# Shorter candidate lists and bf16 steps in the expert routing, forty instead of thirty-two slots taken beside the dense products, one pool to each weight and row buffer

## The chip, the cores and the metric

The kernel runs on one core of one Trainium2 chip. The metric is device time in microseconds (us) of one execution: 1737.02 us, the median of three runs (1736.02 to 1741.25). Smaller is better.

## The reference, cut to what matters

The program is three transformer layers over 256 tokens of width 1024. The change lies wholly in the last sublayer, a product-key expert layer, and in the two pool lines that all layers use:

```python
def peer_ffn(h, w_q, sub_keys, u, v):          # 256 tokens, 8 heads, 128 keys per half, 16384 experts
    q = (hf @ w_q).reshape(n, PEER_HEADS, 2, PEER_HALF)
    sc = jnp.einsum('nhcd,hckd->nhck', q, sub_keys)
    s_top, i_top = lax.top_k(sc, PEER_TOPK)                                   # 16 of 128, per half
    cand_s = s_top[:, :, 0, :, None] + s_top[:, :, 1, None, :]                # 16 x 16 pair sums
    cand_i = i_top[:, :, 0, :, None] * PEER_N_KEYS + i_top[:, :, 1, None, :]
    best_s, pos = lax.top_k(cand_s.reshape(n, PEER_HEADS, 256), PEER_TOPK)    # the 16 best pairs
    best_i = jnp.take_along_axis(cand_i.reshape(n, PEER_HEADS, 256), pos, axis=-1)
    g = jax.nn.softmax(best_s, axis=-1)
    # 128 slots (8 heads x 16) per token; for each token and slot e:
    a = gelu(h . u[e]) * g ;  out = sum over slots of a * v[e]
```

## The kernel before, in words

Everything up to the expert layer is a chain of matrix products whose weights stream from HBM in blocks of 128 x 1024 fp32 (512 KB). `fetch` starts the load of a block into a "raw" buffer from SyncE's queue; `split` makes a rounded copy `whi` on ScalarE (L444) and the rest `wlo` on VectorE (L445, or L293 where VectorE's order is kept); `mm3` (L383 to L385) multiplies both. The raw and `whi`/`wlo` buffers come from two pools that `weight_pools` opens, one with three raw buffers and one with three pairs at the time of the expert layer.

The expert layer (`peer_stage`) has two stages.

**The dense stage.** `nblocks` runs 128 blocks "u" on TensorE: the products of all tokens with all 16384 rows of the table u, laid into a 128 KB per partition `grid` (ScalarE, L1528). After each block `tick` advances two generators by one step each. `paced` advances `routes`: for each of 8 heads `routing` finds the 16 best of 128 for both halves (MAX8, FIND_INDEX8, MATCH_REPLACE8), forms 256 pair sums, takes the 16 best pairs, and turns their positions into key indices by an equality compare, a multiply and a reduce over 1024 elements each (two token halves x 16 picks x 2 halves x 16 candidates); after the eighth head `gates` follows. `two_heads` takes slots 0 to 31 (heads 0 and 1) of the first 128 tokens out of turn: for each slot GpSimd gathers 128 rows of u by index (`row_load`, L1548, one indirect DMA of 512 KB), VectorE forms the dot product, and later the row of v is gathered and added into `peerq`. Row n is due at block 13 + 1.5 n, so 64 rows are spread over blocks 13 to 109. Their buffers are seven quarter rows of the grid that no product has reached yet; four of them are given up at block 96. On VectorE all of this stands in program order (`_InOrder`, L293) with the splits.

**The row stage.** `expert_sums` closes the weight pools and opens its own in their place: six row buffers `vrow` in one pool, then `oj`, `junk` and small tiles. What is left are the v rows of all slots but those 32: 128 loads "o" in groups of four (step n = 0 to 31; each row there is for one slot of 64 tokens twice), 64 loads "u" of token half 1 and 32 of half 0. In step n, `second` builds one-hot columns (L1702 on TensorE, L1704 on VectorE), `weights` picks the dot products out of the grid (L1716 on TensorE, L1722 on VectorE) and applies the gelu, `add` sums four rows on TensorE (L1740); from n = 16 on four "u" units follow, three as a multiply-add on VectorE (L1762), the fourth as a diagonal product on TensorE (ScalarE L1757 makes the diagonal, TensorE L1759). After step 30 `turn(0)` (L1750) makes the weights of half 0, and the last 32 units run, 22 on VectorE and 10 on TensorE. `close` normalizes and writes one token half. Loads are issued by GpSimd in one fixed order, as soon as one of 12 row buffers (two in `xres`, six `vrow`, four in the tiles `xh` and `xl`) is free; eight more come out of the grid after every eighth step.

Of the kernel before, what the change touches and what calls it, by code (L numbers as in the profile page):

```python
# [212 lines left out]

_CONST = [("ident", 128), ("ones", 128), ("iota", 128)]
_CONST2 = [("ones64", 128), ("perm1", 128), ("perm2", 128), ("tri", 128), ("wmask", 256), ("gla", 7 * 128)]


def _constants():
    i = np.arange(128)
    c = {}  # L220
    c["ident"] = np.eye(128)
    c["ones"] = np.ones((128, 128))
    c["iota"] = np.tile(i[None, :], (128, 1))
    c["ones64"] = (i[:, None] // 64 == i[None, :] // 64) * 1.0
# [24 lines left out]
    b = np.concatenate([c[n] for n, _ in _CONST2], axis=1).astype(np.float32)  # L249
    return np.ascontiguousarray(a), np.ascontiguousarray(b)  # L250
# [45 lines left out]
class _Kernel:  # L296
# [355 lines left out]
    def run(self):  # L652
# [16 lines left out]
        nc.vector.memset(self.eps, EPS)  # L669
        self.ident, self.ones, self.iota = c1[:, 0:128], c1[:, 128:256], c1[:, 256:384]  # L670

# [784 lines left out]
    def peer_stage(self):  # L1456
        nc, tc = self.nc, self.tc
        with ExitStack() as s:
# [65 lines left out]
            self.dve = _InOrder(tc, nc.vector)  # L1524
            self.start(self.paced(routes(), 0.68))
            self.start(self.two_heads(p1, base, own, htok, rcol, tok, q, xd))
# [7 lines left out]

    def paced(self, gen, rate):

        n = t = 0
        while True:
            t += 1
            while n < max(min(t, 10), t * rate):  # L1540
                if next(gen, self) is self:
                    return
                n += 1
            yield

    def row_load(self, out, table, idx):

        self.nc.gpsimd.indirect_dma_start(out, None, self.A[table], bass.IndirectOffsetOnAxis(ap=idx, axis=0))  # L1548

    def two_heads(self, p1, base, own, htok, rcol, tok, q, xd):  # L1550


        v = self.dve
        idx = p1.tile([128, 32], U32, name="idx0")
        gate = p1.tile([128, 32], F32, name="gate0")
        a = p1.tile([128, 32], F32, name="act0")
        sm = p1.tile([128, 2], F32, name="gsum0")
        acc = q[:, 0:4].rearrange("p k t -> p (k t)")
# [3 lines left out]
        loaded = ready = 0  # L1562
        first, pace = 13, 1.5

# [3 lines left out]
        def load():  # L1568
            nonlocal loaded
            while loaded < 64:  # L1570
                if loaded < 32 and ready <= loaded // 16:
                    return
                end = first + 1 + pace * loaded
# [4 lines left out]
                n = loaded % 32  # L1578
                self.row_load(at[loaded][1], "pu" if loaded < 32 else "pv", idx[:, n : n + 1])
                loaded += 1  # L1580
# [18 lines left out]

        for n in range(64):  # L1600
            while True:
                prepare()
                if self.scored >= 4 and not begun:
                    begun = True
                    self.nc.gpsimd.dma_start(acc, xd[:, 0:D])
                if block() >= first + pace * n and (ready > n // 16 if n < 32 else self.scored >= 4):
                    break
# [4 lines left out]
            assert block() < end, (n, block(), end)  # L1612
            if n < 32:
                v.scalar_tensor_tensor(row, row, 1.0, htok, op0=OP.mult, op1=OP.mult, accum_out=a[:, n : n + 1])
            else:
                v.scalar_tensor_tensor(acc, row, a[:, n - 32 : n - 31], acc, op0=OP.mult, op1=OP.add)
            if used:
                free.append(used)
            used = end, row
            if n == 31:  # L1620
                v.tensor_scalar(a, a, rcol[:, 0:1], None, op0=OP.mult)
# [4 lines left out]
    def expert_sums(self, s, grid, own, slot, idxp, idxt, jrow, sums, xd):  # L1626
# [144 lines left out]
        for n in range(32):  # L1771
# [11 lines left out]
            if n >= 16:  # L1783
                for k in range(4 * (n - 16), 4 * (n - 16) + 4):
                    unit(1, k, k % 4 == 3)
                    load()
        for k in range(32, 64):
            unit(0, k, k % 3 == 1)
            load()
            if k == 40:  # L1790
                self.close(1, sums, acc[0], free.pop(0))
# [33 lines left out]
    def routing(self, p2, h, q, tok, left):  # L1825

        nc = self.nc
        v = self.dve
# [15 lines left out]
        it = p2.tile([128, 2, 2, 16], U32, tag="rit", bufs=1, name=self.name("rit"))  # L1844
        itf = p2.tile([128, 2, 2, 16], F32, tag="ritf", bufs=1, name=self.name("ritf"))
        for c, tt in pairs:
# [38 lines left out]
        pf = p2.tile([128, 2, 16, 2], F32, tag="pf", bufs=1, name=self.name("pf"))  # L1885
        v.tensor_single_scalar(pij[:, :, :, 0], pos, 4, op=OP.logical_shift_right)
        v.tensor_single_scalar(pij[:, :, :, 1], pos, 15, op=OP.bitwise_and)
        v.tensor_copy(pf, pij)
        yield

        eq = self.x[:, 0:4].rearrange("p n t -> p (n t)")
        v.tensor_tensor(eq.rearrange("p (m b) -> p m b", b=16),
                        pf.rearrange("p t k c -> p (t k c)").unsqueeze(2).broadcast_to([128, 64, 16]),
                        self.iota[:, 0:16].unsqueeze(1).broadcast_to([128, 64, 16]), op=OP.is_equal)
# [81 lines left out]
```

## Time and profile before

| | |
|---|---|
| median of three runs | 1737.02 us |
| profiled execution: its own time / its span | 1743.55 / 1741.8 us |
| dense stage of the expert layer | about 985 to 1358 us of the span |
| row stage | 1358 to 1742 us |
| TensorE busy in the dense / the row stage to 1689 us | 99% / 63% |
| DMA share in the same two | 0.73 / 0.93 |

The profile is that of one execution, which took 6.5 us more than the median. Times in rows are us from the span's start, durations of one instruction ns or us as the row says. Two instructions in a row on VectorE overlap by some 0.08 us, so durations added up come out a few per cent above the time they take. "Remote" and "issue" name idle time of an engine for which the profile shows no releaser.

### The profile page before, as it was taken

What the parts mean: (1) busy time and instruction counts of PE and PEld (TensorE: products, weight loads), DVE (VectorE), ACT (ScalarE), POOL (GpSimd) and SP (SyncE); (2) the same over time, 40 slices, a digit from 0 to 9 for tenths busy, and PEclk for the clock granted to TensorE, in tenths of its full rate; (3) what the DMA queues carried; (4) which work ended last, traced back from release to release, by engine and by line L of the source; (5) the groups of instructions that cost most, each with busy time, mean ns of one, the idle gap of its engine ahead of it and who ended that gap; (6) DMA issues with size and microseconds to landing.
All of it is one profiled execution on the core that took longest, in us unless ns stands there. A gap on an engine that the chain in (4) does not pass through costs nothing.

```text
span 1741.8 us, 31524 instructions
## 1 busy us (share of the span) xinstructions
PE 1568.8 (90%) x12094; PEld 1423.6 (82%) x12094; DVE 1354.2 (78%) x2929; ACT 846.7 (49%) x1522; POOL 340.4 (20%) x313
## 2 busy tenths in 40 slices
PE   6999999999999999999999999999999756674656
PEld 6999999988999999898998999999999534342322
DVE  7859888897788888888776789999994546664657
ACT  7546555755665558348756555555556100000002
POOL 0000000000000000000000043344220466676670
PEclk9999999999999999999999999999999979776868
DMA  6446555424465554443554688877865699998991
GB/s 233 136 146 197 187 185 182 161 96 158 141 199 184 187 188 160 137 145 100 179 180 151 240 329 297 308 252 250 278 232 204 236 348 326 342 356 336 352 377 32
DMA packets 108711, 380.07 MB, mean 218 GB/s; under 512 B 12288, under 2 KB 16896, under 8 KB 108432
## 3 DMA queue, kind: packets, MB, share of 16 engines
q1 hardware_dynamic: 64640, 223.20, 38.6%
q0 software_dynamic: 41760, 152.06, 23.7%
q10 hardware_dynamic: 2160, 2.79, 0.5%
q8 instruction: 95, 1.56, 0.4%
q14 instruction: 56, 0.46, 0.1%
HBM read 375.91 MB, written 2.10 MB: 217 GB/s over the span
## 4 chain that ended last, share of the span: by engine, by line
PE 77%; DVE 11%; issue 5%; another core or an unknown queue 4%; ACT 2%; DMA 1%; DVEq 0%; ACTq 0%
PE mm L383 17%; PE mm L385 17%; PE mm L384 17%; PE acc L384 4%; PE acc L383 4%; PE acc L385 4%; PE mm L1716 3%; DVE junk L1722 3%; DVE peerq L1762 2%; PE acc L1740 2%; PE acc L1759 1%; DVE oj L1704 1%; DVE wlo L293 1%; PE acc L611 1%
## 5 line engine op out<-in xcount | busy, mean ns | idle before, releaser
L383 PE MATMUL mm<-xh,whi 128*128 128x256 f32 x2536 | 724.1, 286 | 5.6 <-DVE z L882 2.7
L385 PE MATMUL mm<-xh,wlo 128*128 128x256 f32 x2536 | 716.8, 283 | 2.2 <-DVE wlo L293 2.1
L384 PE MATMUL mm<-xl,whi 128*128 128x256 f32 x2536 | 717.1, 283 | 0.2 <-DVE xl L492 0.2
L444 ACT CAST whi<-raw 128x1024 fp32r<-128x1024 f32 x366 | 383.1, 1050 | 393.8 <-PE mm L384 197.5
L383 PEld LDWEIGHTS mm<-xh,whi 128*128 128x128 f32 x2536 | 483.2, 191 | 12.7 <-DVE z L882 3.1
L385 PEld LDWEIGHTS mm<-xh,wlo 128*128 128x128 f32 x2536 | 483.6, 191 | 4.3 <-DVE wlo L293 2.9
L384 PEld LDWEIGHTS mm<-xl,whi 128*128 128x128 f32 x2536 | 484.1, 191 | 1.7 <-DVE xl L492 0.6
L445 DVE TENSOR_TENSOR wlo<-raw,whi 128x1024 fp32r<-128x1024 f32 x291 | 354.8, 1223 | 98.0 <-ACT whi L444 95.7
L1716 PE MATMUL mm<-grid,oj 128*128 128x128 f32 x512 | 85.6, 326 | 97.9 <-issue 43.2
L1548 POOL DMA_INDIRECT grid<-in_pu,idx x32 | 50.4, 1574 | 603.5 <-DMA keys<-in_keys 537.6
L1716 PEld LDWEIGHTS mm<-grid,oj 128*128 128x128 f32 x512 | 75.9, 231 | 106.4 <-issue 67.2
L374 ACT ACTIVATE a<-a 128x8 f32<-128x8 f32 x32 | 6.7, 210 | 257.6 <-DVE a L1724 120.3
L1722 DVE SCALAR_TENSOR_TENSOR junk<-c1t,slotT,mm 128x128 f32<-128x128 f32 x256 | 88.7, 346 | 49.7 <-remote 21.1
L293 DVE TENSOR_TENSOR wlo<-raw,whi 128x1024 fp32r<-128x1024 f32 x75 | 91.2, 1222 | 23.7 <-ACT whi L444 23.6
L384 PE MATMUL acc<-fl,whi 128*128 128x256 f32 x352 | 98.9, 281 | 0.1
L385 PE MATMUL acc<-fh,wlo 128*128 128x256 f32 x352 | 98.5, 280 | 0.0
L383 PE MATMUL acc<-fh,whi 128*128 128x256 f32 x352 | 97.7, 279 | 0.0
L1704 DVE TENSOR_SCALAR oj<-mm,cols 128x512 f32<-128x512 f32 x64 | 45.8, 747 | 61.3 <-remote 33.2
L444 ACT CAST whi<-grid 128x1024 fp32r<-128x1024 f32 x51 | 53.8, 1054 | 63.1 <-PE mm L384 51.6
L1528 ACT COPY grid<-mm 128x256 f32<-128x256 f32 x128 | 80.5, 629 | 5.9 <-PE mm L385 5.9
L1548 POOL DMA_INDIRECT grid<-in_pv,idx x32 | 63.0, 1968 | 99.6 <-DVE peerq L293 79.1
L1548 POOL DMA_INDIRECT vrow<-in_pv,idxp x60 | 60.1, 1001 | 68.6 <-PE mm L385 37.4
(415 smaller groups left out, 2748.2 us busy)
## 6 DMA issues: line engine op xcount, KB each, us to landing
raw<-in_wts SPq DMA_DIRECT2D x366, 512.0 KB
grid<-in_wts SPq DMA_DIRECT2D x51, 512.0 KB
mem<-in_mem SPq DMA_DIRECT2D x8, 128.0 KB
xspill<-grid ACTq DMA_DIRECT2D x1, 1024.0 KB
peerq<-xspill POOLq DMA_DIRECT2D x2, 512.0 KB
out<-grid SPq DMA_DIRECT2D x4, 256.0 KB
vrow<-in_pv,idxp POOLq DMA_INDIRECT x60
grid<-in_pv,idxt POOLq DMA_INDIRECT x60
```

What stands on the lines that cost most here:

```text
L293: return lambda *a, **kw: self.tc.keep_in_program_order(f(*a, **kw))
L383: mm(ps, lhsT=wh, rhs=xh, start=first, stop=False, skip_group_check=True)
L384: mm(ps, lhsT=wh, rhs=xl, start=False, stop=False, skip_group_check=True)
L385: mm(ps, lhsT=wl, rhs=xh, start=False, stop=last, skip_group_check=True)
L444: self.nc.scalar.copy(hi, x)
L445: self.dve.tensor_tensor(lo, x, hi, op=OP.subtract)
L1528: lambda i, ps: nc.scalar.copy(grid[:, :, :, :, i // 16, i % 16], ps.rearrange("p (t c r) -> p t c r", t=2, c=8)))
L1548: self.nc.gpsimd.indirect_dma_start(out, None, self.A[table], bass.IndirectOffsetOnAxis(ap=idx, axis=0))
L1704: v.tensor_scalar(oj[:, h], ps, ip, None, op0=OP.is_equal)
L1716: keep(nc.tensor.matmul(ps[:, c].rearrange("p (q i) -> p q i", q=8), lhsT=oj[:, h, c], rhs=grid[:, tt, 2 * c + h, r], start=True, stop=True))
L1722: v.scalar_tensor_tensor(junk, self.iota, slot[:, 0, t : t + 1], bank[h][:, c], op0=OP.is_equal, op1=OP.mult, accum_out=a[:, h, c : c + 1])
L1740: keep(nc.tensor.matmul(acc[n // 16][hf][32 * c : 32 * c + 32], lhsT=strips[n % 3][:, c, 31 - r : 63 - r], rhs=rows[c][:, hf * 512 : hf * ...
```

## The change

Four things change. (1) `routing` forms only the pair sums that can be among the best 16: all 16 partners for the first 4, the first 4 for the other 12, so 112 instead of 256, and the searches read 112. Positions become indices by sums of index steps: `dif` holds the differences of successive indices in bf16, the compare is "position at or past the start of candidate b" against a new constant `cuts` (fp32 in, bf16 out), the multiply and the reduce read bf16. Two conversions leave VectorE, and three stand on ScalarE instead. (2) `two_heads` takes 40 slots in place of 32, 80 rows, one every 1.4 blocks to block 35 and one every 1.08 after that; `paced` gives the routing 0.76 of a step per block, then 0.5, and 1.25 from block 104. The row stage loses 8 units of half 0. Two small tiles move into a constant. (3) Each weight buffer and each `vrow` gets a pool of its own; the `vrow` pools are opened last, so that they lie on the three pairs, and are used in the order in which those come free. (4) Row loads keep their program order on GpSimd.

```diff
     def weight_pools(self, stack, raw_bufs, hl_bufs, side="left"):
-        raw = stack.enter_context(self.tc.tile_pool(name=self.name("wraw"), bufs=raw_bufs, side=side))
-        hl = stack.enter_context(self.tc.tile_pool(name=self.name("whl"), bufs=hl_bufs, side=side))
-        self.wraw = self.wraw + [raw] * raw_bufs
-        self.whl = self.whl + [hl] * hl_bufs
+        for pools, n, name in ((self.wraw, raw_bufs, "wraw"), (self.whl, hl_bufs, "whl")):
+            pools += [stack.enter_context(self.tc.tile_pool(name=self.name(name), bufs=1, side=side)) for _ in range(n)]
...
-            while n < max(min(t, 10), t * rate):
+            while n < max(min(t, 10), min(10 + 0.76 * (t - 10), 29 + 0.5 * (t - 35)), 63.5 + 1.25 * (t - 104)):
...
-        self.nc.gpsimd.indirect_dma_start(out, None, self.A[table], bass.IndirectOffsetOnAxis(ap=idx, axis=0))
+        self.tc.keep_in_program_order(self.nc.gpsimd.indirect_dma_start(
+            out, None, self.A[table], bass.IndirectOffsetOnAxis(ap=idx, axis=0)))
...
-        first, pace = 13, 1.5
+        def when(n):
+            return 13 + 1.4 * n if n < 16 else 35.4 + 1.08 * (n - 16)
...
-        for n in range(64):
+        for n in range(80):
...
-        free = xrows + [pv.tile([128, D], F32, name=f"vrow{i}") for i in range(6)]
+        pw.tile([128, 40], F32, name="pad")
+        vrows = [s.enter_context(tc.tile_pool(name=f"pv{i}", bufs=1, side="right")).tile(
+            [128, D], F32, name=f"vrow{i}") for i in range(6)]
+        free = xrows + [vrows[2 * ((self.wi + j) % 3) + i] for j in range(3) for i in range(2)]
...
-        units = {1: [(1, k) for k in range(64)], 0: [(0, k) for k in range(32, 64)]}
+        units = {1: [(1, k) for k in range(64)], 0: [(0, k) for k in range(40, 64)]}
...
-        for k in range(32, 64):
-            unit(0, k, k % 3 == 1)
+        for k in range(40, 64):
+            unit(0, k, k % 3 == 2)
...
+        dif = p2.tile([128, 2, 2, 16], BF16, tag="rdif", bufs=1, name=self.name("rdif"))
...
-        for tt in range(2):
-            v.tensor_tensor(cand[:, tt].rearrange("p (a b) -> p a b", a=16),
-                            st[:, tt, 0].unsqueeze(2).broadcast_to([128, 16, 16]),
-                            st[:, tt, 1].unsqueeze(1).broadcast_to([128, 16, 16]), op=OP.add)
+        for a0, a1, b1, p0, p1 in ((0, 4, 16, 0, 64), (4, 16, 4, 64, 112)):
+            shape = [128, 2, a1 - a0, b1]
+            v.tensor_tensor(cand[:, :, p0:p1].rearrange("p t (a b) -> p t a b", b=b1),
+                            st[:, :, 0, a0:a1].unsqueeze(3).broadcast_to(shape),
+                            st[:, :, 1, 0:b1].unsqueeze(2).broadcast_to(shape), op=OP.add)
+        cand = cand[:, :, 0:112]
...
-        v.tensor_copy(itf, it)
+        nc.scalar.copy(itf[:, :, :, 1:17], it)
...
+        v.tensor_tensor(dif, itf[:, :, :, 1:17], itf[:, :, :, 0:16], op=OP.subtract)
...
-        v.tensor_copy(pf, pij)
+        nc.scalar.copy(pf[:, :, :, 0], pos)
+        nc.scalar.copy(pf[:, :, :, 1:3], pij)
...
+        v.scalar_tensor_tensor(pf[:, :, :, 2], pf[:, :, :, 0], 64.0, pf[:, :, :, 2], op0=OP.is_ge, op1=OP.mult)
+        v.tensor_tensor(pf[:, :, :, 1], pf[:, :, :, 1], pf[:, :, :, 2], op=OP.subtract)
+        eq = self.x[:, 0:2].rearrange("p n t -> p (n t)").bitcast(BF16)
...
-        v.tensor_tensor(e4, e4, itf.rearrange("p t c b -> p t (c b)").unsqueeze(2).broadcast_to([128, 2, 16, 32]),
+        v.tensor_tensor(e4, e4, dif.rearrange("p t c b -> p t (c b)").unsqueeze(2).broadcast_to([128, 2, 16, 32]),
```

GpSimd's instructions where the dense stage ends, before (`xres`, `vrow` and `grid` are places of row buffers; the buffers `vrow` 16946 to 16951 are the six of the one pool, 16952 and 16953 lie in `xh` and `xl`):

```order
L1765 DMA peerq<-xspill 128x1024
L1548 DMA grid<-in_pv,idx_12255 128x1024 x6
L1548 DMA xres<-in_pv,idxp 128x1024 x2
L1548 DMA vrow_16953<-in_pv,idxp 128x1024
L1647 MEMSET strip_16938 128x252
L1647 MEMSET strip_16939 128x252
L1647 MEMSET strip_16940 128x252
L1548 DMA vrow_16946<-in_pv,idxp 128x1024
```

The same place now (17027 to 17047 are the six `vrow` buffers, a pool each):

```order
L1549 DMA grid<-in_pv,idx_12289 128x1024 x40
L1774 DMA peerq<-xspill 128x1024
L1549 DMA xres<-in_pv,idxp 128x1024 x2
L1652 MEMSET strip_17015 128x252
L1652 MEMSET strip_17016 128x252
L1652 MEMSET strip_17017 128x252
L1549 DMA vrow_17027<-in_pv,idxp 128x1024
```

A row of the twelfth buffer no longer stands ahead of the first `vrow` loads, and the 40 loads of v rows of the dense stage stand in one piece.

VectorE's last units before the second `close`, before:

```order
L1751 SCALAR_TENSOR_TENSOR wsmall<-mm_18960,cols,wsmall 128x64
L1762 SCALAR_TENSOR_TENSOR peerq<-grid,wsmall,peerq 128x1024 x3
L1762 SCALAR_TENSOR_TENSOR peerq<-xres,wsmall,peerq 128x1024
L1802 TENSOR_TENSOR peerq<-peerq,acc_17071 128x512
...
L1762 SCALAR_TENSOR_TENSOR peerq<-grid,wsmall,peerq 128x1024 x14
```

The same now:

```order
L1760 SCALAR_TENSOR_TENSOR wsmall<-mm_19048,cols,wsmall 128x64
L1771 SCALAR_TENSOR_TENSOR peerq<-grid,wsmall,peerq 128x1024 x3
L1771 SCALAR_TENSOR_TENSOR peerq<-xres,wsmall,peerq 128x1024
L1811 TENSOR_TENSOR peerq<-peerq,acc_17167 128x512
...
L1771 SCALAR_TENSOR_TENSOR peerq<-grid,wsmall,peerq 128x1024 x8
```

From the weights of half 0 on, 25 multiply-adds stood on VectorE, and 19 stand there now; six of them are gone from the last run.

## Rows read from the trace of the kernel before

**Rows 1.** Busy time by stretch (length, then busy us and instructions of each engine, then TensorE's granted clock, DMA share and GB/s): the dense stage, 24 us early in it, its blocks 35 to 104, and two parts of the row stage.

```profile
985.00:1358.00 373.00, 370.89 (x3093) 368.30 (x3091) 330.19 (x705) 210.76 (x296) 117.25 (x68) 1.00 0.73 258
1020.00:1044.00 24.00, 24.00 (x202) 24.00 (x202) 22.49 (x62) 12.89 (x17) 9.93 (x7) 1.00 1.03 409
1090.00:1289.00 199.00, 198.12 (x1652) 196.25 (x1651) 195.73 (x416) 110.89 (x148) 77.06 (x44) 1.00 0.78 271
1358.00:1505.00 147.00, 94.76 (x736) 57.42 (x734) 85.71 (x371) 12.41 (x58) 88.97 (x96) 0.86 0.90 326
1505.00:1689.00 184.00, 113.20 (x609) 61.50 (x609) 109.69 (x322) 14.98 (x56) 126.94 (x126) 0.75 0.95 352
```

**Rows 2.** TensorE's waits in the dense stage (us in total, times, longest).

```profile
PE mm L385 <- DVE wlo L293: 2.1, 4, 1.2
```

**Rows 3.** Two splits on VectorE late in the dense stage, where nothing else stands on it (start, us).

```profile
1341.97 1.23 DVE L293 TENSOR_TENSOR wlo<-raw,whi 128x1024 fp32r<-128x1024 f32 x1 [1.66 <-ACT whi L444]
1344.85 1.23 DVE L293 TENSOR_TENSOR wlo<-raw,whi 128x1024 fp32r<-128x1024 f32 x1 [1.65 <-ACT whi L444]
```

**Rows 4.** VectorE's groups in the dense stage by form (count, busy us, mean ns, idle before). FIND_INDEX8, MAX8 and MATCH_REPLACE8 search; 128x256 are the pair sums.

```profile
L293 DVE TENSOR_TENSOR wlo<-raw,whi 128x1024 fp32r<-128x1024 f32 x75 | 91.2, 1222 | 23.7 <-ACT whi L444 23.6
L293 DVE TENSOR_TENSOR wlo<-grid,whi 128x1024 fp32r<-128x1024 f32 x51 | 62.1, 1224 | 5.3 <-ACT whi L444 5.1 <-issue 0.2
L293 DVE SCALAR_TENSOR_TENSOR peerq<-grid,act,peerq 128x1024 f32<-128x1024 f32 x32 | 41.0, 1280 | 0.0
L293 DVE SCALAR_TENSOR_TENSOR grid<-grid 128x1024 f32<-128x1024 f32 x32 | 39.0, 1219 | 0.1
L293 DVE FIND_INDEX8 rit<-rst,xres 128x8 uint32<-128x128 f32 x64 | 17.5, 294 | 0.0
L293 DVE MAX8 rst<-xres 128x8 f32<-128x128 f32 x64 | 14.3, 287 | 5.0 <-ACT xres L1842 5.0
L293 DVE FIND_INDEX8 pos<-xres 128x8 uint32<-128x256 f32 x32 | 13.1, 424 | 0.0
L293 DVE MAX8 xres<-xres 128x8 f32<-128x256 f32 x32 | 12.0, 418 | 0.0
L293 DVE TENSOR_TENSOR xres<-xres,ritf 128x1024 f32<-128x1024 f32 x8 | 9.8, 1220 | 0.0
L293 DVE TENSOR_TENSOR xres<-pf,c1t 128x1024 f32<-128x1024 f32 x8 | 9.8, 1219 | 0.0
L293 DVE TENSOR_REDUCE xres<-xres 128x64 f32<-128x1024 f32 x8 | 9.7, 1216 | 0.0
L293 DVE MATCH_REPLACE8 xres<-rst,xres 128x128 f32<-128x128 f32 x32 | 8.7, 282 | 0.0
L293 DVE MATCH_REPLACE8 xres<-xres 128x256 f32<-128x256 f32 x16 | 6.5, 414 | 0.0
L293 DVE TENSOR_TENSOR xres<-rst 128x256 f32<-128x256 f32 x16 | 6.1, 431 | 0.0
L293 DVE TENSOR_TENSOR xres<-xres,gmx 128x128 f32<-128x128 f32 x2 | 0.6, 292 | 0.1
```

**Rows 5.** GpSimd's row loads around the end of the dense stage, in order of time.

```profile
1317.95 1.27 POOL L1548 DMA_INDIRECT xres<-in_pv,idxp  x1 [26.04 <-PE mm L385]
...
1358.41 0.99 POOL L1548 DMA_INDIRECT vrow<-in_pv,idxp  x1 [37.38 <-PE mm L385]
...
1370.34 0.94 POOL L1548 DMA_INDIRECT vrow<-in_pv,idxp  x1 [0.30 <-issue]
```

**Rows 6.** VectorE at the second step of the row stage, in order of time.

```profile
1366.88 0.17 DVE L1724 TENSOR_TENSOR a<-a,rs 128x8 f32<-128x8 f32 x1
1371.08 0.35 DVE L1722 SCALAR_TENSOR_TENSOR junk<-c1t,slotT,mm 128x128 f32<-128x128 f32 x1 [4.03 <-remote]
```

**Rows 7.** TensorE at the same place: the picks of step 1 and the first sum of rows.

```profile
1364.72 2.05 PE L1716 MATMUL mm<-grid,oj 128*128 128x128 f32 x16 [0.27 <-DVE junk L1722]
1372.11 1.07 PE L1740 MATMUL acc<-xres,strip 128*32 128x512 f32 x2 [5.34 <-issue]
```

**Rows 8.** The largest unexplained waits of the row stage (us in total, times, longest).

```profile
PE mm L1716 <- issue: 43.2, 9, 15.2
...
DVE oj L1704 <- remote: 33.2, 6, 15.9
```

**Rows 9.** VectorE at the end, in order of time: the weights of half 0, the last run of units, the second close.

```profile
1688.83 0.28 DVE L1750 TENSOR_SCALAR wsmall<-mm,cols 128x64 f32<-128x64 f32 x1 [7.64 <-PE acc L1740]
...
1697.47 0.69 DVE L1802 TENSOR_TENSOR peerq<-peerq,acc 128x512 f32<-128x512 f32 x1 [3.01 <-PE acc L1759]
...
1711.35 18.46 DVE L1762 SCALAR_TENSOR_TENSOR peerq<-grid,wsmall,peerq 128x1024 f32<-128x1024 f32 x14
1729.91 1.29 DVE L1802 TENSOR_TENSOR peerq<-peerq,acc 128x512 f32<-128x512 f32 x2
```

**Rows 10.** TensorE at the end: the last two diagonal products.

```profile
1722.81 1.98 PE L1759 MATMUL acc<-grid,wsmall 128*128 128x512 f32 x4 [0.55 <-ACT wsmall L1757]
1725.35 1.98 PE L1759 MATMUL acc<-grid,wsmall 128*128 128x512 f32 x4 [0.55 <-ACT wsmall L1757]
```

**Rows 11.** GpSimd at the end: the first and the last of the final 32 row loads.

```profile
1650.21 0.94 POOL L1548 DMA_INDIRECT xres<-in_pv,idxt  x1 [0.30 <-issue]
...
1694.38 0.94 POOL L1548 DMA_INDIRECT grid<-in_pv,idxt  x1 [0.31 <-issue]
```

More of the change, by code (lines that the diff above doesn't have):

```diff
@@ L210, in _pack_small @@
     return np.ascontiguousarray(np.concatenate([parts[k].astype(np.float32) for k, _ in _SMALL], axis=1))
-_CONST = [("ident", 128), ("ones", 128), ("iota", 128)]
+_CONST = [("ident", 128), ("ones", 128), ("iota", 128), ("cuts", 32)]
 _CONST2 = [("ones64", 128), ("perm1", 128), ("perm2", 128), ("tri", 128), ("wmask", 256), ("gla", 7 * 128)]
@@ L223, in _constants @@
     c["iota"] = np.tile(i[None, :], (128, 1))
+    k = np.arange(16)
+    c["cuts"] = np.tile(np.concatenate([np.where(k < 4, 16 * k, 48 + 4 * k), k])[None, :], (128, 1))
     c["ones64"] = (i[:, None] // 64 == i[None, :] // 64) * 1.0
@@ L669, in run @@
         nc.vector.memset(self.eps, EPS)
-        self.ident, self.ones, self.iota = c1[:, 0:128], c1[:, 128:256], c1[:, 256:384]
+        self.ident, self.ones, self.iota, self.cuts = (c1[:, a:b] for a, b in ((0, 128), (128, 256), (256, 384), (384, 416)))
         with ExitStack() as s1:
@@ L1524, in peer_stage @@
             self.dve = _InOrder(tc, nc.vector)
-            self.start(self.paced(routes(), 0.68))
+            self.start(self.paced(routes()))
             self.start(self.two_heads(p1, base, own, htok, rcol, tok, q, xd))
@@ L1533, in peer_stage, with paced @@
             self.expert_sums(s, grid, own, slot, idxp, idxt, jrow, q.rearrange("p (t k) n -> p t (k n)", t=2), xd)
-    def paced(self, gen, rate):
+    def paced(self, gen):
         n = t = 0
@@ L1546, in row_load @@
     def row_load(self, out, table, idx):
-        self.nc.gpsimd.indirect_dma_start(out, None, self.A[table], bass.IndirectOffsetOnAxis(ap=idx, axis=0))
+        self.tc.keep_in_program_order(self.nc.gpsimd.indirect_dma_start(
+            out, None, self.A[table], bass.IndirectOffsetOnAxis(ap=idx, axis=0)))
     def two_heads(self, p1, base, own, htok, rcol, tok, q, xd):
         v = self.dve
[L1554 to L1557, printed above, removed]
+        idx = p1.tile([128, 48], U32, name="idx0")
+        gate, a, sm = self.ones[:, 0:48], self.ones[:, 48:96], self.ones[:, 96:99]
         acc = q[:, 0:4].rearrange("p k t -> p (k t)")
@@ L1569, in load @@
             nonlocal loaded
-            while loaded < 64:
-                if loaded < 32 and ready <= loaded // 16:
+            while loaded < 80:
+                if loaded < 40 and ready <= loaded // 16:
                     return
-                end = first + 1 + pace * loaded
+                end = when(loaded) + 1
                 k = next((k for k, (b, _) in enumerate(free) if end < b), None)
@@ L1577, in load @@
                 at[loaded] = free.pop(k)
-                n = loaded % 32
-                self.row_load(at[loaded][1], "pu" if loaded < 32 else "pv", idx[:, n : n + 1])
+                n = loaded % 40
+                self.row_load(at[loaded][1], "pu" if loaded < 40 else "pv", idx[:, n : n + 1])
                 loaded += 1
@@ L1587, in prepare @@
             h = ready
-            if h == 2 or self.heads <= h:
+            if h == 3 or self.heads <= h:
                 return
@@ L1605, in two_heads @@
                     self.nc.gpsimd.dma_start(acc, xd[:, 0:D])
-                if block() >= first + pace * n and (ready > n // 16 if n < 32 else self.scored >= 4):
+                if block() >= when(n) and (ready > n // 16 if n < 40 else self.scored >= 4):
                     break
@@ L1612, in two_heads @@
             assert block() < end, (n, block(), end)
-            if n < 32:
+            if n < 40:
                 v.scalar_tensor_tensor(row, row, 1.0, htok, op0=OP.mult, op1=OP.mult, accum_out=a[:, n : n + 1])
             else:
-                v.scalar_tensor_tensor(acc, row, a[:, n - 32 : n - 31], acc, op0=OP.mult, op1=OP.add)
+                v.scalar_tensor_tensor(acc, row, a[:, n - 40 : n - 39], acc, op0=OP.mult, op1=OP.add)
             if used:
@@ L1619, in two_heads @@
             used = end, row
-            if n == 31:
+            if n == 39:
+                a, gate = a[:, 0:40], gate[:, 0:40]
                 v.tensor_scalar(a, a, rcol[:, 0:1], None, op0=OP.mult)
@@ L1844, in routing @@
         it = p2.tile([128, 2, 2, 16], U32, tag="rit", bufs=1, name=self.name("rit"))
-        itf = p2.tile([128, 2, 2, 16], F32, tag="ritf", bufs=1, name=self.name("ritf"))
+        if h == 0:
+            self.itf = p2.tile([128, 2, 2, 17], F32, tag="ritf", bufs=1, name="ritf")
+            v.memset(self.itf[:, :, :, 0:1], 0.0)
+        itf = self.itf
+        dif = p2.tile([128, 2, 2, 16], BF16, tag="rdif", bufs=1, name=self.name("rdif"))
         for c, tt in pairs:
@@ L1884, in routing @@
         pij = p2.tile([128, 2, 16, 2], U32, tag="pij", bufs=1, name=self.name("pij"))
-        pf = p2.tile([128, 2, 16, 2], F32, tag="pf", bufs=1, name=self.name("pf"))
-        v.tensor_single_scalar(pij[:, :, :, 0], pos, 4, op=OP.logical_shift_right)
-        v.tensor_single_scalar(pij[:, :, :, 1], pos, 15, op=OP.bitwise_and)
-        v.tensor_copy(pf, pij)
-        yield
[L1891 to L1894, printed above, removed]
+        v.tensor_single_scalar(pij[:, :, :, 0], pos, 15, op=OP.bitwise_and)
+        v.tensor_single_scalar(pij[:, :, :, 1], pos, 12, op=OP.bitwise_and)
+        pf = self.x[:, 2, 128:224].rearrange("p (t k c) -> p t k c", t=2, c=3)
+        nc.scalar.copy(pf[:, :, :, 0], pos)
+        nc.scalar.copy(pf[:, :, :, 1:3], pij)
+        yield
+        v.scalar_tensor_tensor(pf[:, :, :, 2], pf[:, :, :, 0], 64.0, pf[:, :, :, 2], op0=OP.is_ge, op1=OP.mult)
+        v.tensor_tensor(pf[:, :, :, 1], pf[:, :, :, 1], pf[:, :, :, 2], op=OP.subtract)
+        eq = self.x[:, 0:2].rearrange("p n t -> p (n t)").bitcast(BF16)
+        v.tensor_tensor(eq.rearrange("p (k c b) -> p k c b", c=2, b=16),
+                        pf[:, :, :, 0:2].rearrange("p t k c -> p (t k) c").unsqueeze(3).broadcast_to([128, 32, 2, 16]),
+                        self.cuts.rearrange("p (c b) -> p c b", c=2).unsqueeze(1).broadcast_to([128, 32, 2, 16]),
+                        op=OP.is_ge)
         yield
         e4 = eq.rearrange("p (t k m) -> p t k m", t=2, k=16)
-        v.tensor_tensor(e4, e4, itf.rearrange("p t c b -> p t (c b)").unsqueeze(2).broadcast_to([128, 2, 16, 32]),
+        v.tensor_tensor(e4, e4, dif.rearrange("p t c b -> p t (c b)").unsqueeze(2).broadcast_to([128, 2, 16, 32]),
                         op=OP.mult)
```

5 lines of the change are left out of this document (2 added, 3 removed).

## The prediction

> **What bounds the kernel now.** I read busy time by stretch first [rows 1], since the change touches two stages with different limits. In the dense stage TensorE is busy 370.9 of 373 us at full clock, and its only wait is 2.1 us for a split [rows 2]: it is bound by TensorE. One block takes 2.88 us (two splits late in the stage are that far apart [rows 3]), so 128 blocks end at 1358 us and begin near 989; blocks 35 to 104 are the stretch 1090 to 1289. VectorE is close behind there, 195.7 of 199 us [rows 1]: what is added to it in that stretch can surface, what is added elsewhere has room (330.2 of 373 us busy).
>
> The row stage is another matter. TensorE is busy 63% of it, VectorE 59%, the DMA engines 90 to 95% [rows 1]. The loads run at 326 and 352 GB/s, while 409 GB/s were moved early in the dense stage, so the DMA engines are nearly, not wholly, the limit. The engines' own chain stops now and then, up to 15.9 us at a time, for nothing that the profile names [rows 8]. After the last load, issued at 1694.4 [rows 11], what ends last is not a transfer: the multiply-adds of half 0 can start only with its weights at 1688.8, and VectorE works through them until 1729.9, when the second close begins [rows 9].
>
> **The change part by part.** All terms are against the profiled execution, 1743.55 us, of which 1741.8 are its span; the median of the runs lies 6.5 us lower, and I move the sum to it unchanged.
>
> *The end, minus 7.6 us.* The last run on VectorE is 14 units in 18.46 us, 1.32 each [rows 9]. Eight units leave half 0, of which VectorE had six (22 of 32 before, 16 of 24 now): 6 x 1.32 = 7.9 us, so VectorE would be free at 1722.0. But the second close also needs the diagonal products, of which two go (10 before, 8 now). They stand 2.54 us apart (1722.81 and 1725.35), the last ends at 1727.3 [rows 10], and 2 x 2.54 takes that to 1722.2. So TensorE is late next by 0.2 us, and 7.7 of the 7.9 us come through; I take 7.6 for the hand-over between the two. ScalarE's diagonal is inside the 2.54.
>
> *The start of the row stage, minus 4 us.* Before, the six `vrow` buffers waited as one for the last product: their first load goes out at 1358.4 and nine more follow in one piece until 1371.3 [rows 5]. Now buffer pair one waits for block 125 alone, pair two for block 126. With blocks of 2.88 us that is 1352.4 and 1355.2: four loads go out before the stage begins. The first sum of rows started at 1372.1, after 5.3 us of waiting, though its picks had ended at 1366.8 [rows 7]. At most that is won, 5.3 us. Whether the rows or VectorE made it wait the trace leaves open: VectorE itself stood 4.0 us until 1371.1 without a named cause [rows 6], and if that has nothing to do with the ten loads, nothing is won. The pause lies wholly inside the stretch in which GpSimd issues without a gap, and that stretch loses its first four loads, so I take 4.0, near the upper end; 0 and 5.3 are the ends.
>
> *Fewer loads, minus 1 us.* Eight rows of 0.524 MB at 352 GB/s [rows 1] are 12 us of transfer that leave the end. Since the end goes by VectorE's chain, the last load may land 12 us earlier without moving it. What can follow is a shorter pause: the first close waits 3.0 us for a product [rows 9], in the stretch where the loads run without a gap. I take 1 of these 3. Upper end: if the loads set the time at which the weights of half 0 are ready, the 7.6 us that VectorE waited for it [rows 9] fall too, 10.6 in all; lower end 0.
>
> *The dense stage, plus 1 us.* On VectorE, per head: four FIND_INDEX8 and four MAX8 go from 256 to 112 wide, priced by the 128-wide rows, 4 x (424 - 294) + 4 x (418 - 287) = 1.04 us; two MATCH_REPLACE8 2 x (414 - 282) = 0.26; two sums 2 x (431 - 292) = 0.28 [rows 4]. Two small new instructions cost at most 0.29 each; two casts leave and a subtraction of the same width comes, which I call even. That is 1.0 us less per head, 8.0 in all. The multiply and the reduce over 1024 elements, now in bf16, are not in the trace; between no gain and half of their 1.22 us [rows 4] they give 0 to 9.8 us, so 8.0 to 17.8 us go. The compare reads fp32 and stays at 1.22.
>
> The page "VectorE: DVE Perf Modes" of the Trainium skill says, in its section "The perf-mode tier table (the rule you actually need)", that a tensor_tensor doubles its rate when all its operands are 16 bits wide, and that tensor_reduce has only the single rate in any type. By that the multiply halves and the reduce stays, and the bf16 buys half of what its form suggests, 4.9 us; the rows of before, all fp32 and all at 1.22, cannot tell. By this rule the dense term would be 2 us in place of 1.
>
> What comes: 16 rows, half as dot products of 1.219 and half as sums of 1.280 [rows 4], 20.0 us, and a third head's gate, four small instructions. So VectorE does 3 to 13 us more in a stage in which it has 43 us of room, most of it after block 109. What counts is the middle, blocks 35 to 104. Before, a block held one split (1.22), 1/1.5 of a row at 1.25 (0.83), and 0.68 of a routing step. A step is 1.21 us: 330.2 busy, less splits (153.3) and rows (80.0), over 80 steps [rows 1, 4]; 0.82 per block. Sum 2.87. Now: 1.22, 1.25/1.08 = 1.16, and 0.5 x (96.9 - 8.0 to 17.8)/80 = 0.49 to 0.56: 2.87 to 2.94. The same load that TensorE covered with 2.1 us of waits, or up to 0.07 x 69 = 5 us over. I take 1; the ends are -2 (the old waits vanish) and +5. A dot product that waits for its row holds the splits queued behind it on VectorE, and TensorE waits for these. ScalarE gets three short copies per head and is busy 57% [rows 1]; GpSimd's 16 more loads find it busy 117 of 373 us.
>
> The DMA engines carry more there too: 44 loads on GpSimd between 1090 and 1289 [rows 1] become 64, 10.5 MB more in 199 us, 324 in place of 271 GB/s, by the same share per GB/s 0.93 in place of 0.78. The 409 GB/s beside a TensorE at full pace [rows 1] say that it fits.
>
> *Nothing* for the separate weight pools elsewhere: the buffers are taken in the same turn as before.
>
> Sum: -7.6 - 4.0 - 1.0 + 1.0 = -11.6 us, 1743.55 to 1731.95 for an execution like the profiled one, 1737.0 to **1725.4 us** by the median.
>
> **Rivals.**
>
> *Only the end counts.* The pause before the first sum of rows stays, and the four early loads wait in their buffers. For it: VectorE's wait names no load. Time: 1737.0 - 7.6 + 1.0 = 1730.4 us.
>
> *The row stage is bound by its transfers after all.* At a share of 0.90 to 0.95 [rows 1] that is possible. Then every load not made there counts: 8 gone and 4 made earlier, each 336 us / 222 loads = 1.51 us (224 less the two early ones into `xres`; from 1358.4 to the last issue at 1694.4), 18.2 us: 1737.0 - 18.2 + 1.0 = 1719.8 us. Against it: the weights of half 0 come long after their rows were asked for.
>
> *A pause more or less.* The unnamed pauses are up to 15.9 us long [rows 8], and shifted instructions may gain or lose one: 1741 or 1710 us.
>
> *The dense stage starves (the slower side).* 69 weight blocks and 64 rows, with the weights loaded ahead as before, are 324 GB/s x 199 us = 64.4 MB. If the DMA engines don't sustain more than 297 GB/s, halfway from the measured 271 to the wanted 324, the stretch takes 217 us: rows come late, VectorE stands before them with the splits behind it, TensorE stops. Plus 18 on the other terms: 1737.0 - 12.6 + 18 = 1742.4 us. It decides from 324 GB/s downwards, and reaches slower than before below 300. For it: a share of 0.93 is what the row stage has at its limit. Against it: 409 GB/s for 24 us.
>
> **How the numbers follow.** The forecast as it stands has 40%, only the end 20%, bound by transfers 20%, a pause more or less 6% each, starvation 8%. The bounds of the forecast's own terms add up to -7.6 - 5.3 - 10.6 - 2 = -25.5 and -7.6 + 5 = -2.6 us, 1711.5 to 1734.4; they take in the next two rivals. Leaving out most of the pause lost or gained and of starvation, I state 1710 to 1736 us. Within 0.3% (5.2 us, about what a measurement of this kernel can tell from no change) lies 1731.8 to 1742.2. Faster: nearly all of the forecast (38), two thirds of only the end (13), all of the transfers' case (20), a pause less (6): 0.77. Slower: half of starvation and, for causes I have no row for, some more: 0.09. Within: 0.14.
>
> **What would show it.** The end: 19 multiply-adds after the weights of half 0, a last run of 8, and the second close about 33 us after these weights where it was 41. The start: `vrow` loads about 6 and 3 us ahead of the last product, and the first sum of rows within 1 to 2 us of its picks. The dense stage: TensorE's waits still under 5 us, the multiply near 0.65 us and the reduce at 1.2 or near 0.65, some 324 GB/s between blocks 35 and 104, no wait of VectorE for a gathered row. The forecast is wrong if TensorE waits more than 5 us in the dense stage, if the weights of half 0 do not come earlier than 331 us after the dense stage ends, or if the pauses add up to something else than before.

## The result and the profile after

The kernel after takes 1715.94 us (median of six runs, 1710.25 to 1726.30), the kernel before 1737.27 us beside it: a ratio of 0.9879, 95% interval 0.9851 to 0.9907. That is 21.3 us, where 11.6 were forecast. The profiled execution of after is its slowest (1726.30 us, span 1724.5), so the spans differ by 17.3 us. Four times read from the timelines split them: ScalarE's first and last copy of a dense block into the grid (their ends), the weights of half 0, the second close.

| stretch, us | before | after | difference | forecast |
|---|---|---|---|---|
| start to first dense block | 986.3 | 982.1 | -4.3 | 0 |
| first to last dense block | 372.6 | 372.2 | -0.4 | +1 |
| to the weights of half 0 | 329.9 | 325.4 | -4.5 | -4 |
| to the second close | 41.1 | 33.6 | -7.5 | -7.6 - 1 |
| rest | 11.9 | 11.3 | -0.6 | 0 |

Busy time by stretch in after, as [rows 1] (length, busy us and instructions of TensorE, its weight loads, VectorE, ScalarE, GpSimd, then clock, DMA share, GB/s):

```profile
1090.00:1289.00 199.00, 197.94 (x1670) 196.50 (x1669) 193.74 (x380) 114.37 (x162) 95.74 (x57) 1.00 0.88 316
1358.00:1505.00 147.00, 94.54 (x716) 58.64 (x716) 86.58 (x376) 11.65 (x56) 83.94 (x90) 0.84 0.87 317
1505.00:1689.00 184.00, 113.12 (x602) 58.56 (x595) 112.38 (x317) 17.18 (x62) 119.68 (x118) 0.76 0.91 344
```

The middle blocks move 316 GB/s in place of 271, and the row stage looks as it did. But TensorE issues 1670 products where before had 1652 in the same 199 us, though it was busy for 198 of them both times. Counted off by the block products (each trace has 3049 of them), the first 35 blocks went from 101.6 to 105.0 us, blocks 35 to 104 from 203.1 to 198.5, the rest from 71.1 to 71.9: the -0.4 of the stage is a sum of gains and losses.

VectorE's groups in the dense stage by form, as [rows 4] (count, busy us, mean ns, idle):

```profile
L296 DVE TENSOR_TENSOR xres<-xres,c1t 128x1024 bf16<-128x1024 f32 x8 | 9.8, 1225 | 0.3
L296 DVE TENSOR_REDUCE xres<-xres 128x64 f32<-128x1024 bf16 x8 | 9.7, 1215 | 0.0
L296 DVE TENSOR_TENSOR xres<-xres,rdif 128x1024 bf16<-128x1024 bf16 x8 | 5.5, 684 | 0.0
```

The multiply on bf16 alone takes 684 ns, the reduce 1215 and the compare 1225: bf16 buys 4.3 us.

TensorE's waits in the dense stage, as [rows 2], and VectorE's only wait there for a gathered row:

```profile
PE mm L386 <- DVE wlo L296: 1.8, 3, 0.8
PE acc L1962 <- ACT xres L1951: 1.1, 1, 1.1
PE mm L384 <- issue: 0.9, 1, 0.9
PE mm L384 <- ACT grid L1529: 0.6, 2, 0.4
...
DVE peerq L296 <- DMA grid<-in_pv,idx: 1.8, 1, 1.8
```

GpSimd's loads around the end of the dense stage (last block 1354.3), as [rows 5], and TensorE's first sum of rows, as [rows 7], in order of time:

```profile
1348.32 0.94 POOL L1549 DMA_INDIRECT vrow<-in_pv,idxp  x1 [0.15 <-issue]
...
1351.05 0.94 POOL L1549 DMA_INDIRECT vrow<-in_pv,idxp  x1 [0.54 <-PE mm L386]
...
1353.90 0.94 POOL L1549 DMA_INDIRECT vrow<-in_pv,idxp  x1 [0.67 <-PE mm L386]
...
1363.50 0.58 PE L1711 MATMUL mm<-jrow,idb 128*128 128x128 bf16 x4 [5.38 <-DVE oj L1713]
...
1367.87 1.02 PE L1749 MATMUL acc<-xres,strip 128*32 128x512 f32 x2
```

The pairs of loads go out some 6 and 3 us ahead of the last block, as said. Yet the first sum comes 13.6 us behind it, where before it was 13.2: the sum no longer waits behind its picks, but the picks come later.

The end, as [rows 9, 10], on VectorE (weights, last run, second close) and TensorE (last diagonal product):

```profile
1679.66 0.28 DVE L1759 TENSOR_SCALAR wsmall<-mm,cols 128x64 f32<-128x64 f32 x1 [5.45 <-PE acc L1768]
...
1702.61 10.53 DVE L1771 SCALAR_TENSOR_TENSOR peerq<-grid,wsmall,peerq 128x1024 f32<-128x1024 f32 x8
...
1711.54 1.99 PE L1768 MATMUL acc<-grid,wsmall 128*128 128x512 f32 x4 [0.55 <-ACT wsmall L1766]
...
1713.25 1.29 DVE L1811 TENSOR_TENSOR peerq<-peerq,acc 128x512 f32<-128x512 f32 x2
```

The last run is 8 units, and TensorE ends just beside VectorE. The pauses without a named cause stayed, as [rows 8]; all of VectorE's of that kind in the row stage (1358 to 1689 us) come to 79.1 us, before to 83.4:

```profile
DVE oj L1713 <- remote: 46.3, 4, 15.7
PE mm L1725 <- issue: 41.6, 16, 15.9
```

### The profile page after: what moved, and what is told of

The parts are those of the page before. It is cut to its first block, busy times and chain, and to the rows that moved or that the text cites. A ratio compares the mean times of both kernels' runs of the same rounds, so it can differ in the third digit from the quotient of the medians.

```text
span 1724.5 us, 31581 instructions
## 1 busy us (share of the span) xinstructions
PE 1559.0 (90%) x12086; PEld 1414.9 (82%) x12086; DVE 1348.2 (78%) x2960; ACT 849.1 (49%) x1546; POOL 349.2 (20%) x321
## 4 chain that ended last, share of the span: by engine, by line
PE 78%; DVE 9%; issue 5%; ACT 3%; another core or an unknown queue 2%; DMA 2%; POOL 0%; ACTq 0%; DVEq 0%; POOLq 0%; SPq 0%
PE mm L384 17%; PE mm L386 17%; PE mm L385 17%; PE acc L385 4%; PE acc L386 4%; PE acc L384 4%; PE mm L1725 4%; PE acc L1749 2%; DVE peerq L1771 2%; DVE junk L1731 2%; DVE oj L1713 1%; ACT whi L445 1%; PE acc L1768 1%; PE mm L1711 1%
## 5 line engine op out<-in xcount | busy, mean ns | idle before, releaser
L384 PEld LDWEIGHTS mm<-xh,whi 128*128 128x128 f32 x2536 | 478.4, 189 | 14.0 <-DVE fpad L848 3.1
L386 PEld LDWEIGHTS mm<-xh,wlo 128*128 128x128 f32 x2536 | 478.5, 189 | 4.0 <-DVE wlo L296 2.6
L385 PEld LDWEIGHTS mm<-xl,whi 128*128 128x128 f32 x2536 | 479.1, 189 | 2.1 <-DVE xl L493 0.7
L1549 POOL DMA_INDIRECT grid<-in_pu,idx x40 | 63.3, 1582 | 603.4 <-DVE c1t L296 533.6
L1731 DVE SCALAR_TENSOR_TENSOR junk<-c1t,slotT,mm 128x128 f32<-128x128 f32 x256 | 88.6, 346 | 35.6 <-remote 13.3
L296 DVE TENSOR_TENSOR wlo<-raw,whi 128x1024 fp32r<-128x1024 f32 x75 | 91.4, 1220 | 22.1 <-ACT whi L445 20.6
L1549 POOL DMA_INDIRECT grid<-in_pv,idx x40 | 68.3, 1708 | 69.6 <-DVE peerq L296 58.1
L385 PEld LDWEIGHTS acc<-fl,whi 128*128 128x128 f32 x352 | 66.3, 188 | 0.8 <-DVE fl L446 0.7
```

What stands on the lines that cost most here:

```text
L296: return lambda *a, **kw: self.tc.keep_in_program_order(f(*a, **kw))
L384: mm(ps, lhsT=wh, rhs=xh, start=first, stop=False, skip_group_check=True)
L385: mm(ps, lhsT=wh, rhs=xl, start=False, stop=False, skip_group_check=True)
L386: mm(ps, lhsT=wl, rhs=xh, start=False, stop=last, skip_group_check=True)
L1549: self.tc.keep_in_program_order(self.nc.gpsimd.indirect_dma_start(out, None, self.A[table], bass.IndirectOffsetOnAxis(ap=idx, axis=0)))
L1731: v.scalar_tensor_tensor(junk, self.iota, slot[:, 0, t : t + 1], bank[h][:, c], op0=OP.is_equal, op1=OP.mult, accum_out=a[:, h, c : c + 1])
```

## The experiments

The kernel before took 1674.3 us beside e1 to e8, and 1736.5 and 1734.5 us beside e9 to e11 and e12, so comparisons go by the ratio to it. The difference lies in the row stage: in e1 to e8 VectorE shows no wait on "remote" there, and the loads run at 387 to 404 GB/s from 1358 to 1505 us (317 above, 323 to 333 in e9 to e12). I call these the chip without and with pauses. All four times are read as above, from one profile a run.

| run | ratio to before (95%) | first block | dense stage | to weights | to close |
|---|---|---|---|---|---|
| e2 before + pools | 0.9985 (0.9976 to 0.9994) | 986.0 | 372.2 | 242.3 | 55.5 |
| e5 before + 32 columns | 0.9971 (0.9960 to 0.9982) | 982.0 | 371.5 | 244.7 | 57.2 |
| e3 after, 32 slots | 0.9924 (0.9911 to 0.9938) | 982.0 | 365.5 | 244.1 | 55.0 |
| e4 after, old routing | 0.9967 (0.9955 to 0.9980) | 981.8 | 382.0 | 243.8 | 45.8 |
| e1 after, one vrow pool | 0.9881 (0.9865 to 0.9898) | 982.1 | 368.8 | 245.2 | 45.6 |
| e7 after | 0.9867 (0.9853 to 0.9882) | 981.5 | 369.4 | 244.0 | 43.3 |
| e6 after, narrow constants | 0.9896 (0.9881 to 0.9910) | 986.1 | 371.4 | 243.1 | 42.7 |
| e8 after + 8 columns | 0.9855 (0.9841 to 0.9869) | 980.1 | 368.6 | 244.5 | 43.5 |
| with pauses: e9 fp32 picks | 0.9898 (0.9867 to 0.9929) | 982.0 | 374.7 | 317.3 | 29.5 |
| e10 narrow + 8 columns | 0.9846 (0.9815 to 0.9877) | 979.1 | 369.7 | 313.7 | 35.5 |
| e11 four products fewer | 0.9931 (0.9903 to 0.9959) | 981.9 | 370.8 | 313.6 | 39.7 |
| e12 before + 8 columns | 0.9944 (0.9917 to 0.9971) | 979.0 | 371.5 | 318.7 | 49.1 |

**The parts taken out one at a time.** e1:

```diff
-        vrows = [s.enter_context(tc.tile_pool(name=f"pv{i}", bufs=1, side="right")).tile(
-            [128, D], F32, name=f"vrow{i}") for i in range(6)]
+        pv = s.enter_context(tc.tile_pool(name="pv", bufs=1, side="right"))
+        vrows = [pv.tile([128, D], F32, name=f"vrow{i}") for i in range(6)]
```

> The kernel after, with its six vrow buffers in one pool again (the weight pools stay apart). The prediction's theory: the early loads are worth 4 us (0 to 5.3), so about 1720 us, the first vrow load again goes out only after the last product, and the first sum of rows starts some 5 us after its picks. If the row stage is bound by its transfers, four loads at 1.51 us come back late: 1722 us. If the early loads only wait in their buffers: 1716 us.

e2 is before with the pool lines of the diff (`weight_pools`, `vrows`, `pad`).

> The kernel before, with the pools of the change alone (a pool to each weight buffer and to each vrow). The prediction's theory: 1737 less 4, 1733 us, all of it after the last product; the stretches before the dense stage keep their times. The rival that the profile of after raised: the dense stage began 3.8 us earlier there, with an even gain from 30 us to 700 us (172 matmuls per 20 us where before had 170.5); if the weight pools give that, it is here too, the casts at 680 us come 4 us earlier than before, and the time is 1729 us. If neither holds: 1737 us.

e3 is after with `two_heads` and `paced` of before, and at the end:

```diff
-        for k in range(40, 64):
-            unit(0, k, k % 3 == 2)
+        for k in range(32, 64):
+            unit(0, k, k % 3 == 1)
```

> The kernel after, with 32 slots in the dense stage again and 32 units of half 0 at the end (routing and pools of after). The prediction's theory: 7.6 us come back at the end and 1 us of the first close, the dense stage loses its rows' load and gives back 1 us: 1723 us, and the second close 41 us after the weights of half 0. If the transfers bound the row stage: eight loads at 1.51 us, 1728 us, the weights of half 0 later by up to 4 us after the last product. If dense rows cost what they save: 1716 us.

e4 is after with `routing` of before.

> The kernel after, with the routing of before (256 pair sums, picks in fp32), forty slots and pace kept. The prediction's working gives VectorE 1.22 + 1.16 + 0.61 = 2.99 us per block in blocks 35 to 104 against TensorE's 2.88: TensorE waits 0.11 x 69 = 7.6 us more in the dense stage, 1723 us. The rival: VectorE catches up where the pace leaves room, and the routing is worth nothing: 1716 us.

e7 is after, unchanged.

> The kernel after, unchanged, beside the others. If the vrow buffers of their own matter as predicted, it is 4 us under the kernel with one vrow pool (ratio 0.9881 there), 0.986; if the early loads only wait in their buffers, 0.988. Where the row stage runs without the long unnamed pauses, its end should wait for loads (1.2 us before each pair of multiply-adds), as in the first four runs.

Against e7 (1652.4 us) the vrow pools are worth 2.5 us (not clear of noise: the intervals of e1 and e7 overlap; e2, with the weight pools too, gains 2.5 by its ratio, and its interval stays below 1), the slots 8.1, the routing 16.1, twice the 7.6 expected. With the 5.1 of the place (below) that is 31.8 us, where the whole change is worth 21.9 here: the parts are not independent, since the slots spend time that the routing frees. In e1 and in e7 the first sum of rows starts 8.2 us after the last block: the early loads don't bring it forward. From e1 to e7 the profiles gain most in the last column (2.3 us), where VectorE waits for rows. e7's last units, in order of time:

```profile
1629.17 2.60 DVE L1771 SCALAR_TENSOR_TENSOR peerq<-grid,wsmall,peerq 128x1024 f32<-128x1024 f32 x2 [1.23 <-DMA grid<-in_pv,idxt]
1633.00 2.60 DVE L1771 SCALAR_TENSOR_TENSOR peerq<-grid,wsmall,peerq 128x1024 f32<-128x1024 f32 x2 [1.23 <-DMA grid<-in_pv,idxt]
1636.78 1.28 DVE L1771 SCALAR_TENSOR_TENSOR peerq<-grid,wsmall,peerq 128x1024 f32<-128x1024 f32 x1 [1.18 <-DMA grid<-in_pv,idxt]
```

Each wait names a load: without pauses the end goes by the transfers, and eight loads fewer are 55.0 - 43.3 = 11.7 us, 1.46 each. The slots cost 3.9 us of that in the dense stage (365.5 to 369.4), none of it in blocks 35 to 104 (199.3 to 198.5 us): the first 35 go from 100.5 to 103.8. The routing is no free rider: with 32 slots it shortens the dense stage by 6 us (e5 to e3, which differ in the pools too), with 40 by 12.6 (e4 to e7). The stretch 1090 to 1289 us of e3, of e4, then of e7, as [rows 1]:

```profile
1090.00:1289.00 199.00, 199.00 (x1683) 197.98 (x1682) 190.27 (x426) 115.62 (x174) 68.27 (x41) 1.00 0.79 272
```

```profile
1090.00:1289.00 199.00, 196.00 (x1625) 192.62 (x1625) 195.94 (x355) 108.13 (x142) 99.61 (x58) 1.00 0.87 309
```

```profile
1090.00:1289.00 199.00, 199.00 (x1683) 197.99 (x1682) 195.38 (x392) 113.57 (x162) 94.39 (x57) 1.00 0.87 314
```

Read the products, not the busy time: 1625 in e4, 1683 in e3 and e7. VectorE's busy time doesn't tell either, 195.9 us in e4 and 195.4 in e7. The products' starts do. One block product starts 118.7 to 118.9 ns after the one before it in e3, e4, e5 and e7 (mean of the distances under 130 ns; 120.0 in before). What the dense stage takes beyond that, in longer distances and around the routing's own products, is 13.3 us in e5, 8.1 in e3, 25.2 in e4 and 11.5 in e7 (11.3 in before, 14.9 in after). So the relief of VectorE is a relief of stops of TensorE: 5.2 of the 6 us and all of the 12.6.

**The place of the tiles.** e1, e3 and e4 all start the dense stage some 4 us early, e2 doesn't; of what they share, the width of the constants' tile (`cuts` adds 32 columns) moves every tile behind it. e5 does that alone in before (its edit below; the gates move into the ones to make room), e6 takes it back in after:

```diff
-        c1 = cp.tile([128, 384], F32, name="c1t")
+        c1 = cp.tile([128, 416], F32, name="c1t")
```

> The kernel before, with nothing of the change but the width of the constants' tile (416 columns, as after; the new 32 hold nothing, and the gates take columns of the ones to make the room). Theory of the place: the tile moves every tile behind it by 128 bytes, and that is what lets TensorE issue 172 in place of 170.5 products per 20 us: the dense stage begins at 974.5 in place of 978.5 us, takes some 370 in place of 372.4 us, and the time is 6 us under that of before (ratio 0.9965). The rival, that the faster pace comes from something else in the change: ratio 1.000, dense stage from 978.5.

> The kernel after, with the constants' tile back at 384 columns and the 32 new columns in a small tile of the dense stage. Theory of the place: the dense stage begins 4 us later, at 978.5, and lasts 2 us longer; the time is 6 us over that of the kernel after in this batch. The rival: no difference.

e5 is 5.1 us under before, e6 5.1 us over e7, both with the 4 us ahead of the dense stage: shown from both sides. e8 is after with 424 columns, e10 is e6 with 392, e12 is before with 392.

> The kernel after, with the constants' tile 8 columns wider still (424; the last 8 hold nothing), so that the tiles behind move by 32 bytes more. If the place decides by its distance to the weights or by a boundary, the products per 20 us between 160 and 240 us differ from the 172 of after in either direction, by up to the 0.8% that 128 bytes made, which is 6 to 10 us; if it is not the place, nothing changes.

> The kernel with the narrow constants' tile again, 8 columns wider (392; the last 8 hold nothing): the tiles behind stand 32 bytes above the kernel before's place, 96 below after's. Of the places so far before's gives 119.7 ns a product between 160 and 240 us, after's 119.1, and 32 bytes above after's 118.4. If the place counts within a period of 128 bytes, this one equals the last (118.4 ns, dense stage from 972.5 us, ratio 0.9855); if it goes evenly with the distance, it lies between before and after (119.5 ns, from 977 us, 0.989).

> The kernel before with one edit, the constants' tile 392 columns wide in place of 384 (the last 8 hold nothing): every instruction stands as before, the tiles behind the constants stand 32 bytes higher. Theory of the place: 683 products in 160 to 240 us where before has 676, the dense stage begins near 971.5 in place of 978.6 us and ends some 9 us earlier, TensorE being paced by VectorE in part of it; 7 to 10 us under before, ratio 0.994 to 0.996 on either chip. The rival, that the faster pace of the last two kernels came from their chip or from what else they changed: 1.000.

The stretch 160 to 240 us, far ahead of the expert layer, in before and then in e12:

```profile
160.00:240.00 80.00, 80.00 (x676) 80.00 (x675) 64.73 (x103) 44.87 (x66) 0.00 (x0) 1.00 0.56 185
```

```profile
160.00:240.00 80.00, 80.00 (x683) 80.00 (x683) 65.77 (x105) 45.55 (x66) 0.00 (x0) 1.00 0.57 186
```

Both are busy for all 80 us at full clock, and e12 does 1% more products. In the order of the place, against before's: 0 bytes 675 to 676, 32 bytes 683 (e10, e12), 128 bytes 679 (after), 160 bytes 681 (e8); from start to start these are 118.9, 117.4, 118.2 and 117.9 ns, 0.5 to 0.9 less than the expectation of e10 gives for three of them. Neither expectation is met: growth is not even, and a period of 128 bytes would make 679 equal to 676. e12 changes no instruction and wins 0.56%, most of it ahead of the dense stage, which takes 371.5 us against 372.6: there its products start 117.2 ns apart in place of 120.0, but 18.6 us go beyond that in place of 11.3, VectorE being as busy as before. e8 and e10 have the lowest ratios, but their intervals overlap those of after (e7, and the result above).

**The bf16 steps and the end.** In e9 `dif` and `eq` are fp32 (`dif` and `pf` move to make room):

```diff
-        eq = self.x[:, 0:2].rearrange("p n t -> p (n t)").bitcast(BF16)
+        eq = self.x[:, 0:4].rearrange("p n t -> p (n t)")
```

> The kernel after, with the comparison's result and the index steps in fp32 (112 pair sums stay): the multiply goes back from 684 to about 1225 ns, 0.54 x 8 = 4.3 us more on VectorE in the dense stage. If VectorE's work paces the blocks there, as the 16 us for the whole routing suggest, 3 to 5 us come through: ratio to before 0.989 where after has 0.9867. If the 16 us are the 112 sums' doing alone, by steps that TensorE waits for, nothing: 0.9867.

The time alone doesn't settle it (its interval holds after's ratio). The dense stage points to the stated size: 374.7 us against 370.8 in e11 and 372.2 in after, which have the same dense stage on such a chip, so 2.5 to 3.9 of the 4.3 us; with one profile each that is not settled.

e11 leaves TensorE four of the eight diagonal products:

```diff
-            unit(0, k, k % 3 == 2)
+            unit(0, k, k % 6 == 5)
```

> The kernel after, with 4 of the 24 units of half 0 by TensorE's diagonal products in place of 8, the other 4 by VectorE. The prediction's theory of the end (VectorE's multiply-adds set it): 4 x 1.32 = 5.3 us slower, ratio 0.990. If the loads set it, as the waits of 1.2 us before each pair of multiply-adds say (20 x 1.32 = 26 us of work in the 43 us from the weights of half 0 to the second close): nothing, 0.9867.

With pauses the last load goes out within 12 us of the weights of half 0 (34 to 50 us behind them without), and VectorE's multiply-adds set the end: 39.7 us to the second close, against 29.5, 33.6 and 35.5 in the three profiles with eight diagonal products on such a chip. VectorE is busy 32.7 of these 39.7 us, and 27.5 to 27.6 in each of the three: the 5.1 us of four multiply-adds, while the rest are waits that vary. By its ratio e11 loses some 9 us to after where 5.3 were expected, with intervals that just overlap. e11's last run ends right at the close and waits for nothing:

```profile
1687.51 5.24 DVE L1771 SCALAR_TENSOR_TENSOR peerq<-vrow,wsmall,peerq 128x1024 f32<-128x1024 f32 x4
1692.79 13.17 DVE L1771 SCALAR_TENSOR_TENSOR peerq<-grid,wsmall,peerq 128x1024 f32<-128x1024 f32 x10
1706.06 1.29 DVE L1811 TENSOR_TENSOR peerq<-peerq,acc 128x512 f32<-128x512 f32 x2
```

## Why the prediction was right in sign and short in size

- **The end, -7.6: right.** 41.1 to 33.6 us, TensorE just beside VectorE; VectorE's busy time in it fell by 7.6 us, 35.2 to 27.6, and e11 supports the cause. It holds where the pauses delay the weights. Where they are absent the rival "bound by its transfers" holds, and its 1.51 us a load measured 1.46.
- **The start of the row stage, -4: the size is near, the mechanism failed.** The failed step is that the ten loads hold up the first sum: in after it came 13.6 us behind the last block in place of 13.2, and without pauses at 8.2 us with one pool as with six (e1, e7; 9.1 in e5, before's order). The prediction's own lower end, that VectorE's pause has nothing to do with the loads, is what happened. What the pools give, 2.5 us in e1 and e2, would fit loads made earlier, the transfers' rival, but no run shows it. The -4.5 us of the profile is about what VectorE's idle time without a named cause lost by itself, 83.4 to 79.1 us: kernels with after's order of row-stage work need 313.6 to 325.4 us there, those with before's 318.7 and 329.9, and without pauses it is 244.0 in e7 and 244.7 in e5. So the size is near by luck.
- **Fewer loads, -1.** The first close waits less for its product, 0.5 and 1.0 us in place of 3.0, but VectorE's other pauses there hide whether that reaches the end.
- **The dense stage, +1: near by luck.** Two steps failed. One is "it is bound by TensorE" with 2.1 us of waits to win: VectorE's load did stop TensorE, which the busy time and the waits hardly show, and its relief was worth 6 us and, with forty slots, 12.6. The other is "what is added elsewhere has room": blocks 35 to 104, which were to bear the cost, got 4.6 us faster, and the slots' 3.9 us fell before and after them. The place of the tiles, which the forecast left out, is in this term too: 120.0 to 118.7 ns a product is 4 us over the stage. By the Trainium skill's page "VectorE: DVE Perf Modes", section "The perf-mode tier table (the rule you actually need)", the multiply had to double its rate and the reduce not to; 1220 to 684 ns and 1216 to 1215 ns agree, the first not to the full.
- **"Nothing" elsewhere: wrong, the missing term.** Not the weight pools (e2 begins the dense stage at 986.0) but the wider constants' tile, 5.1 us by e5 and e6, of which 4 fall before the dense stage. That is about half of the shortfall of 9.7 us. The rest is not settled: the row stage up to the weights of half 0 varies by 12 us between profiles of one order. Without pauses the change is worth 21.9 us as well, but by other parts: the end goes by loads there.
- **Starvation: no.** 316 GB/s where 324 were counted, and one wait of 1.8 us for a row.

## What to carry to other kernels

Compare how many products TensorE issues in a stretch, not how long it is busy: 1625 and 1683 in the same 199 us both read as bound by TensorE (196 and 199 us busy). A tile that only grows moves all tiles behind it, so price a layout shift by a kernel with that shift alone. And name the limit of the end stage from its waits on the chip at hand, since the same kernel was bound by loads where there were no pauses (e7) and by VectorE where there were (after).

## What the runs showed of the hardware that was not expected

A shift of the tiles in SBUF by 32 bytes, with every instruction as before, raised TensorE's pace by 1% (676 to 683 products in 80 us, 118.9 to 117.4 ns from one start to the next) at the same granted clock, 1.00; which tile's place counts was not tried. One program ran 3.6% shorter beside e1 to e8 (1674 against 1737 us), nearly all of it where gathered rows fill the DMA engines: 402 GB/s without pauses in e1 against 317 with pauses of up to 16 us in after. What pauses the engines there stays open; the profile names no releaser, and no run isolates it.
